# Two hybrid blocks on one core: the first block's attention turns its probabilities two query tiles behind the scores instead of one

## The chip, the cores and the metric

The kernel runs on one core of one Trainium2 chip. The metric is the device time of one execution in microseconds (us). Each time quoted as a median comes from several executions; the profile comes from one further execution, and has its own time. The engines of a core are called PE (TensorE, with PEld for its weight loads), DVE (VectorE), ACT (ScalarE), POOL (GpSimd) and SP (SyncE, which issues the DMAs). Each engine works through its own queue in order, and waits at the head of it for what the instruction needs.

## The reference, cut to what matters

The program is a block of two layers (`first_block`) followed by a second block with a recurrent part, two attentions and 32 experts. The change lies in the attention of the first block, which each of its two layers runs once, on 528 positions, 4 heads, without a mask:

```python
def mla_mix(c_q, c_kv, k_r, q_norm_w, w_uq, kv_norm_w, w_ukv, cos, sin):
    ...
    def attend(qb):
        s = jnp.einsum('bqhd,bkhd->bhqk', qb, k).astype(jnp.float32) * scale
        p = jax.nn.softmax(s, axis=-1).astype(v.dtype)
        return jnp.einsum('bhqk,bkhd->bqhd', p, v)
...
mix = jnp.concatenate([y_f * silu(f_gate), y_p * silu(p_gate), y_a * silu(a_gate)], axis=-1)
h = h + mix @ w_out[l]
```

A query and a key have 192 numbers for each head (128 of its own and 64 turned by position), a value has 128. Everything is float32.

## The kernel before

**Precision.** A product in float32 is made of three matmuls (`mm3`, L183 to L185): each operand is split into a high and a low part (`split`: ACT copies to the high part at L196, DVE subtracts at L197), and the products high x high, high x low and low x high are added up in PSUM. So each split tile is ready twice: the high part when ACT is done, the low part one DVE instruction later.

**One layer** (`layer`, L323) makes the input projections, then the attention, then the output projection. The attention loops over 4 heads `h` and, for each, over query tiles `i` of 128 positions: five tiles in layer 0 (528 positions, the last tile has 16) and four in layer 1 (512 positions).

- `scores` (L489) writes one tile's scores with ten matmuls (L183 to L185, and L498, L499 for the turned half) into a `pp` tile in PSUM; there are two `pp` buffers. DVE takes the maximum (L501, L502), ACT the exponential (L504), DVE the reciprocal and the product (L506, L507), which gives the probabilities `e` in a slab of SBUF. The `pp` buffer is free again when ACT has read it.
- `transpose_p` (L512) turns `e` with five transposes on PE (L523) into the PSUM tile `pt`, of which there is **one** buffer, and splits it into `pth` and `ptl` (a `big` tile; L196, L197). The next tile can be turned when DVE has read `pt`.
- `outputs` (L529) multiplies the turned probabilities of two or three query tiles with the values, 15 matmuls into a `p1` tile, and gates the result into `ys` (L536). It runs after query tile 1 (part 0) and after the last one (part 1).
- `finish` (L611) is `transpose_p` and, where due, `outputs`, and at a head's end the split of `ys` into `mix[4 + h]`.

**What fills the gaps.** A list of generators, `fillers`, holds independent work of the layer: the query and key projections of the next heads (`qk`), and the gates and the Fourier and pooling mixes (`a_gate`, `fp_gate`). `fill(n)` draws n steps from it; how many after each score tile is a table (`STEPS_1`, L63). After the last head `fill(100)` draws the rest. Then the output projection starts: for each of its 8 column tiles it takes `mix` in the order 2, 0, 4, 5, 6, 1, 3, 7, so that `mix[7]`, the last head's, comes last.

**What sets the order.** The program order is that of the Python code, but the framework's scheduler sorts the instructions of each engine once, at build time, by their place in the code and by its own guess of when they are ready. On the chip each queue then runs strictly in that order.

Of the kernel before, what the change touches and what calls it, by code (L numbers as in the profile page):

```python
# [127 lines left out]
def body(ctx, tc, a, out, stop=None, dbg=None):  # L128
# [61 lines left out]
    def slab(dt=F32, n=L):  # L190
        return sl.tile([128, L + 16], dt, name="slab")[:, :n]
# [23 lines left out]
    with ExitStack() as c1:  # L215
# [7 lines left out]
        def ppt():  # L223
            return pp.tile([128, 2, 512], F32, name="pp")

        def ptt():
            return pt_.tile([128, 1024], F32, name="pt")

        def p1t():
            return p1_.tile([128, 512], F32, name="p1")  # L230
# [92 lines left out]
        def layer(l, w0, X, acc, after):  # L323
# [111 lines left out]
            def a_gate(h):  # L435
                t = slab(n=LQ)
                sa[h] = t
                yield from gate_g(1728 + 128 * h, t)
                a_done[h] = True
# [35 lines left out]
            def qk(h):  # L475
                hp, r, r2 = h // 2, slice(64 * (h % 2), 64 * (h % 2) + 64), slice(64 - 64 * (h % 2), 128 - 64 * (h % 2))
                wq = weights(3, [(0, uq[:, 192 * h:192 * h + 128])])
                wk = weights(2, [(0, ukv[:, 256 * h:256 * h + 128])])
                qh, ql = slab(F32R, LQ), slab(F32R, LQ)
                yield from proj_g(wq, Q, lambda p, f: split(p, f(qh), f(ql)))  # L480
                kf = slab()
                yield from proj_g(wk, KV, lambda p, f: V.tensor_tensor(f(kf), p, f(Rkv), op=OP.mult))
                kh, kl = split(kf)
                qs = slab(F32R, LQ)
                ACT(qs[r], qr[hp][r], AF.Copy)
                V.tensor_tensor(qs[r2], qr[hp][r], qs[r].bitcast(F32), op=OP.subtract)
                heads[h] = (qs, qh, ql, kh, kl)
# [24 lines left out]
            def transpose_p(h, i, e):  # L512
                t0, n = TQ[i]
                part = int(t0 >= 256)
                nq = LQ - 256 if part else 256
                if (h, part) not in pts:
                    pts[h, part] = big.tile([128, 2720], F32R, name="big")
                pt = pts[h, part]
                pth = pt[:, :5 * nq].rearrange("p (j q) -> p j q", j=5)
                ptl = pt[:, 1360:1360 + 5 * nq].rearrange("p (j q) -> p j q", j=5)  # L520
                t = ptt()
                for j, (k0, _) in enumerate(TK):
                    nc.tensor.transpose(t[:106, j * 128:j * 128 + n], e[:n, k0:k0 + 106], ident[:n, :n])  # L523
                tv = t[:106, :640].rearrange("p (j q) -> p j q", j=5)[:, :, :n]
                qo = slice(t0 - 256 * part, t0 - 256 * part + n)
                split(tv, pth[:106, :, qo], ptl[:106, :, qo])
                return pth, ptl
# [10 lines left out]
            def fp_gate(m):  # L538
                yield from (fourier, fourier, pool, pool)[m](m % 2)
                t = slab(n=LQ)  # L540
                yield from gate_g(256 + 128 * m if m < 2 else 768 + 128 * (m - 2), t)
                V.scalar_tensor_tensor(t, yf[m][:, q0:], 0.5, t, op0=OP.mult, op1=OP.mult)
                mix[m] = split(t, n=LQ)
# [7 lines left out]
            for m in range(2):  # L551
                p = ptt()
# [9 lines left out]
            for m in range(2):  # L562
# [7 lines left out]
                p = ppt()  # L570
# [18 lines left out]
            for j, (t0, n) in enumerate(TK):  # L589
                p = p1t()  # L590
# [7 lines left out]
            for pr in range(2):  # L598
                for i, nm in enumerate(("c64", "s64")):
# [5 lines left out]

            fillers.extend([qk(1), fp_gate(0), qk(2)] + [a_gate(2), fp_gate(2)][::2 * l - 1]
                           + [qk(3), a_gate(3), fp_gate(1), fp_gate(3)])
            prev = None
            ys = {}

            def finish(h, i, e):  # L611
                pth, ptl = transpose_p(h, i, e)
                if i in (1, NT - 1):
                    fill()
                    if h not in ys:
                        while not a_done[h]:
                            fill()
                        ys[h] = slab(n=LQ)
                    outputs(h, int(i > 1), pth, ptl, ys[h])
                    if i == NT - 1:  # L620
                        mix[4 + h] = split(ys[h], n=LQ)

            for h in range(4):
                for i in range(NT):
                    while h not in heads:
                        fill()
                    e = scores((h, i, heads[h]))
                    fill(int(STEPS_1[l][h][i]))
                    if prev is not None:
                        finish(*prev)  # L630
                    prev = (h, i, e)
            fill(100)
            wo = w_rows(l, 0)
            finish(*prev)

            order = (2, 0, 4, 5, 6, 1, 3, 7)
            for m in range(8):
# [55 lines left out]
    with ExitStack() as c2:  # L693
# [359 lines left out]
        prev = None  # L1053
        for h in range(8):
# [4 lines left out]
            for i in range(4):  # L1059
                e = scores(h, i)  # L1060
# [5 lines left out]
                prev = (h, i, e)  # L1066
# [86 lines left out]
        prev = None  # L1153
        for h in range(4):
            if h < 3:
                fillers.append(q_head(h + 1))
            for i in range(4):
                e = xscores(h, i)
# [5 lines left out]
                prev = (h, i, e)  # L1164
# [33 lines left out]
        for t in range(len(ring) - 4, len(ring)):  # L1198
            q, e, hf = ring[t][0]
# [494 lines left out]
    with tc.manual_schedule(engines={mybir.EngineType.PE}):  # L1694
# [6 lines left out]
        h = combine(0, up_products(0, "u"), s_)  # L1701
        hT_ = None
        for pr in range(1, NP):
# [38 lines left out]
            h = combine(pr, up_products(pr, "u"), s_)  # L1742
            if pr == NP - 2:

                fnw = wk_.tile([128, 4 * GE * CAP], F32, name="sel")[:, :D]
                for c in range(2):
                    p = ptt()
# [135 lines left out]
```

## Time and profile before

| | us |
|---|---|
| median of 3 executions (1424.39 to 1425.71) | 1425.4 |
| the profiled execution, its own time | 1425.72 |
| its span, first to last instruction | 1423.9 |
| PE busy in the span | 1353.4 (95%) |
| DVE, ACT, POOL busy | 683.4, 555.1, 440.1 |
| attention of layer 0 in the trace | from about 117 to 232 |
| attention of layer 1 in the trace | from about 376 to 481 |

A matmul's bar in the trace is longer than its share of PE, since matmuls overlap: bars of about 0.28 us start about 0.12 us apart. Where the trace prints a wait in brackets, it counts from the modelled end of the matmul before, so the start is later than it would have been by about 0.15 us more than the figure in brackets.

### The profile page before, as it was taken

The page shows a single profiled execution, that of the slowest core. Times are in us where ns is not written, and L with a number is a line of the kernel's source. Part 1 is how long each engine was busy: PE and PEld are TensorE (multiplying, and loading weights), DVE is VectorE, ACT ScalarE, POOL GpSimd, SP SyncE. Part 2 cuts the span into 40 slices and gives each one's busy share as a digit, 9 for nine tenths or more (in the row PEclk, how much of TensorE's full clock was granted, in tenths as well). Part 3 has the DMA queues.
Part 4 walks back from the last instruction along what each step waited for, and adds up shares of the span by engine and source line. Part 5 has one row for each costly group of instructions (what it writes and reads, how often), then busy time and mean ns, then how long its engine had stood idle before and what let it go on. Part 6 is the DMA issues. An engine that isn't in the chain of part 4 may idle for free.

```text
span 1423.9 us, 21255 instructions
## 1 busy us (share of the span) xinstructions
PE 1353.4 (95%) x8236; PEld 1018.1 (71%) x8236; DVE 683.4 (48%) x1305; ACT 555.1 (39%) x1048; POOL 440.1 (31%) x363
## 2 busy tenths in 40 slices
PE   6999999999999999989999999979999999999996
PEld 5998999999899997767876788863454354354343
DVE  5656775455677636777766244252213123132224
ACT  5355554334555562667755344421111110111113
POOL 3432223743222488464477432512000000000002
PEclk9999999999999999999999999989999999999998
DMA  6321112332211242313345122959999999999994
GB/s 202 96 75 40 49 52 84 97 97 66 56 42 58 69 125 81 90 52 120 103 127 175 38 63 91 347 200 382 423 403 423 422 422 423 422 420 422 422 418 154
DMA packets 159288, 279.32 MB, mean 196 GB/s; under 512 B 15568, under 2 KB 127440, under 8 KB 135120
## 3 DMA queue, kind: packets, MB, share of 16 engines
q1 hardware_dynamic: 159184, 277.92, 53.0%
q8 instruction: 66, 1.08, 0.3%
q14 instruction: 38, 0.31, 0.1%
HBM read 275.79 MB, written 2.10 MB: 195 GB/s over the span
## 4 chain that ended last, share of the span: by engine, by line
PE 59%; DVE 7%; DMA 3%; ACT 2%; issue 1%; POOL 1%; DVEq 0%; SPq 0%; POOLq 0%; ACTq 0%
PE pga L1530 7%; PE pgb L1530 7%; PE pm L184 5%; PE pm L185 5%; PE pm L183 5%; PE pgs L1621 4%; PE pgz L1580 3%; PE pgy L1580 3%; PE pgs L1352 3%; PE p L183 2%; PE p L184 2%; PE p L185 2%; DMA ring<-in_expert_gate_w_dram 1%; DMA ring<-in_expert_up_w_dram 1%; DVE slab L197 1%
## 5 line engine op out<-in xcount | busy, mean ns | idle before, releaser
L177 POOL TENSOR_TENSOR wl<-wraw,wh 128x512 fp32r<-128x512 f32 (+1 forms) x248 | 328.1, 1332 | 457.1 <-ACT wh L176 425.2
L176 ACT ACTIVATE wh<-wraw 128x512 fp32r<-128x512 f32 (+1 forms) x248 | 150.6, 616 | 212.6 <-PE pm L184 49.8
L183 PE MATMUL pp<-slab,wh 128*128 128x264 f32 (+1 forms) x536 | 154.8, 290 | 7.6 <-ACT wh L176 6.8
L184 PE MATMUL pp<-slab,wh 128*128 128x264 f32 (+1 forms) x536 | 155.7, 291 | 2.9 <-DVE slab L204 2.7
L185 PE MATMUL pp<-slab,wl 128*128 128x264 f32 (+1 forms) x536 | 154.8, 289 | 1.0 <-POOL wl L177 1.0
L1788 POOL TENSOR_TENSOR ring<-xtok,sel 128x512 f32<-128x512 f32 x4 | 5.0, 1282 | 406.2 <-DVE xtok L1623 406.2
L185 PE MATMUL pm<-slab,wl 128*128 128x512 f32 (+1 forms) x320 | 121.5, 381 | 5.6 <-POOL wl L177 5.5
L184 PE MATMUL pm<-slab,wh 128*128 128x512 f32 (+1 forms) x320 | 120.9, 378 | 2.2 <-DVE slab L197 2.2
L183 PE MATMUL pm<-slab,wh 128*128 128x512 f32 (+1 forms) x320 | 121.1, 380 | 0.0
L183 PE MATMUL p<-slab,wh 128*128 128x264 f32 (+1 forms) x400 | 115.7, 289 | 3.3 <-DVE rs L247 1.6
L1530 PE MATMUL pga<-ring,xT 128*64 128x512 f32 x504 | 116.1, 596 | 0.0
L1530 PE MATMUL pgb<-ring,xT 128*64 128x512 f32 x512 | 113.7, 592 | 0.3 <-DMA ring<-in_expert_up_w_dram 0.3
L185 PE MATMUL p<-slab,wl 128*128 128x264 f32 (+1 forms) x400 | 113.1, 283 | 0.0
L184 PE MATMUL p<-slab,wh 128*128 128x264 f32 (+1 forms) x400 | 112.8, 282 | 0.0
L183 PEld LDWEIGHTS pp<-slab,wh 128*128 128x128 f32 x536 | 103.6, 194 | 8.0 <-ACT wh L176 6.8
L184 PEld LDWEIGHTS pp<-slab,wh 128*128 128x128 f32 x536 | 103.4, 193 | 4.7 <-DVE slab L204 4.2
L185 PEld LDWEIGHTS pp<-slab,wl 128*128 128x128 f32 x536 | 103.8, 194 | 1.5 <-POOL wl L177 1.5
L1530 PEld LDWEIGHTS pgb<-ring,xT 128*64 128x64 f32 x512 | 37.0, 137 | 73.6 <-issue 71.4
L1590 DVE SCALAR_TENSOR_TENSOR yl<-pgy,wcol,yh 128x512 fp32r<-128x512 f32 x16 | 12.0, 751 | 158.2 <-ACT yh L1589 158.2
L1530 PEld LDWEIGHTS pga<-ring,xT 128*64 128x64 f32 x504 | 35.4, 137 | 66.1 <-issue 65.6
L183 PEld LDWEIGHTS p<-slab,wh 128*128 128x128 f32 x400 | 75.5, 189 | 5.1 <-issue 1.7
L184 PEld LDWEIGHTS p<-slab,wh 128*128 128x128 f32 x400 | 75.4, 189 | 0.0
(412 smaller groups left out, 3007.6 us busy)
## 6 DMA issues: line engine op xcount, KB each, us to landing
ring<-in_expert_gate_w_dram SPq DMA_DIRECT2D x63, 1024.0 KB, 17.7
ring<-in_expert_up_w_dram SPq DMA_DIRECT2D x62, 1024.0 KB, 16.2
ring<-in_expert_down_w_dram SPq DMA_DIRECT2D x56, 1024.0 KB, 17.0
wraw<-in_w_in_dram SPq DMA_DIRECT2D x108, 256.0 KB, 2.9
wraw<-in_w_out_dram SPq DMA_DIRECT2D x48, 256.0 KB, 2.9
wraw<-in_xk_w_dram SPq DMA_DIRECT2D x16, 256.0 KB, 2.9
wraw<-in_xv_w_dram SPq DMA_DIRECT2D x16, 256.0 KB, 2.6
wraw<-in_xq_w_dram SPq DMA_DIRECT2D x16, 256.0 KB, 2.9
```

The lines of the kernel that those rows point to most:

```text
L176: ACT(h, raw, AF.Copy)
L177: G.tensor_tensor(lo, raw, h.bitcast(F32), op=OP.subtract)
L183: mm(ps, lh, rh, start=first, stop=False)
L184: mm(ps, lh, rl, start=False, stop=False)
L185: mm(ps, ll, rh, start=False, stop=last)
L197: V.tensor_tensor(lo, x, h.bitcast(F32), op=OP.subtract)
L1352: mm(p, h3[:, i, 128 * k:128 * k + 128], sl_[i], start=i == 0 and z == 0, stop=i == 3 and z == 1)
L1530: mm(p[64 * z:64 * z + 64], xt[:, k, CAP * (q + z):CAP * (q + z) + 64], W(src, 2 * pr + z, k), start=k == 0, stop=k == KT - 1)
L1580: mm(ps[c // 512][64 * z:64 * z + 64, c % 512:c % 512 + n], hT_[:, k, 64 * z:64 * z + 64], W("d", 2 * pr + z, k, c, n), start=k == 0, stop ...
L1590: V.scalar_tensor_tensor(yl, p, w[:rows, 0:1], yh.bitcast(F32), op0=OP.mult, op1=OP.subtract)
L1621: mm(p, t[:, 128 * i:128 * i + 128], y, start=q == 0, stop=q == len(ys) - 1)
L1788: G.tensor_tensor(y[i][:, :512], xtok[:, i, :512], fnw[:, :512], op=OP.mult)
```

## The change

The loop over query tiles kept one finished score tile back (`prev`) and called `finish` on it after the next tile's scores. Now `prev` is a list that keeps two tiles back: `finish` is called on tile n after the scores of tile n + 2, over the heads' borders too. After the last head's scores and `fill(100)` two tiles are left to finish instead of one. Nothing is computed otherwise, and no buffer is added.

```diff
-            prev = None
+            prev = []
...
                     e = scores((h, i, heads[h]))
                     fill(int(STEPS_1[l][h][i]))
-                    if prev is not None:
-                        finish(*prev)
-                    prev = (h, i, e)
+                    prev.append((h, i, e))
+                    if len(prev) > 2:
+                        finish(*prev.pop(0))
             fill(100)
             wo = w_rows(l, 0)
-            finish(*prev)
+            for p in prev:
+                finish(*p)
```

The built order of POOL and of SP is the same before and after. On PE, DVE and ACT it differs only inside the two attentions; from the output projections on, and in the whole second block, it is the same. Three places follow, each with PE's order before and after. Numbers behind a tile's name count the tiles of a program, so they differ between the two; what counts is which instruction stands behind which.

**Layer 0, from head 0 to head 1.** Before, PE's queue after the scores of head 1's second query tile (`pp_1787`): five transposes of head 0's last tile (16 positions), twelve matmuls of a key projection (`p1_1731`, `p1_1739`), then the scores of the third tile (`pp_1825`).

```order
L499 MATMUL pp_1787<-slab_777,slab_1499 128x264
L523 MATMUL pt_1747<-tab_63,slab_1657 106x16 x5
L183 MATMUL p1_1731<-slab_467,wh_1674 128x264
...
L185 MATMUL p1_1739<-slab_538,wl_1675 128x264
L183 MATMUL pp_1825<-slab_1495,slab_1407 128x264
```

After, the same score tiles are `pp_1747` (second), `pp_1816` (third) and `pp_1910` (fourth):

```order
L523 MATMUL pt_1739<-tab_63,slab_1561 106x128 x5
L185 MATMUL pp_1747<-slab_1486,slab_1408 128x264
...
L499 MATMUL pp_1747<-slab_777,slab_1490 128x264
L183 MATMUL pp_1816<-slab_1486,slab_1407 128x264
...
L499 MATMUL pp_1816<-slab_777,slab_1490 128x264
L523 MATMUL pt_1782<-tab_63,slab_1648 106x16 x5
L183 MATMUL pp_1910<-slab_1486,slab_1407 128x264
```

Three score tiles now follow each other, with ten transposes and no key projection between them; the key projection stands ahead of them.

**Layer 1, head 1.** Before, PE's queue around the turning of head 1's third tile (`pt_5109`): 15 matmuls of head 1's first output part (`p1_5026`) and the pooling mix (`p1_5061`) stand ahead of it, and a gate projection (`p1_5080`) behind.

```order
L184 MATMUL p1_5026<-big_4965,big_4453 128x256
L185 MATMUL p1_5026<-big_4965,big_4454 128x256
L183 MATMUL p1_5061<-slab_5007,slab_4509 128x256
L184 MATMUL p1_5061<-slab_5008,slab_4509 128x256
L185 MATMUL p1_5061<-slab_5007,slab_4509 128x256
L523 MATMUL pt_5109<-tab_63,slab_4988 106x128 x2
L183 MATMUL p1_5080<-slab_2815,wh_4914 128x256
```

After, the second tile is turned into `pt_5067` and the third into `pt_5155`; `pp_5108` and `pp_5163` are the scores of head 2's first and second tile:

```order
L498 MATMUL pp_5108<-slab_3914,slab_4878 128x264
L499 MATMUL pp_5108<-slab_3915,slab_4878 128x264
L523 MATMUL pt_5067<-tab_63,slab_4862 106x128 x5
L183 MATMUL pp_5163<-slab_4874,slab_4768 128x264
L523 MATMUL pt_5155<-tab_63,slab_4979 106x128 x2
L183 MATMUL p1_5054<-slab_2815,wh_4885 128x256
```

Two turnings now stand with a single matmul between them, and the first output part comes behind both.

**Layer 0, the end of the attention.** Before, PE's queue behind the last output part of the last head (`p1_2732`): matmuls of the output projection (`pp_2765`, `pp_2833`) with parts of `mix` that are ready, until `slab_2749`, the high part of `mix[7]`, is read.

```order
L185 MATMUL p1_2732<-big_2657,big_1319 128x272
L183 MATMUL pp_2765<-slab_2700,wh_2714 128x264
...
L184 MATMUL pp_2833<-slab_2486,wh_2755 128x264
L183 MATMUL pp_2765<-slab_2749,wh_2720 128x264
L185 MATMUL pp_2833<-slab_2485,wl_2756 128x264
```

After:

```order
L185 MATMUL p1_2732<-big_2695,big_1319 128x272
L185 MATMUL pp_2833<-slab_2691,wl_2756 128x264
L183 MATMUL pp_2765<-slab_2749,wh_2712 128x264
L183 MATMUL pp_2833<-slab_2749,wh_2761 128x264
L184 MATMUL pp_2765<-slab_2750,wh_2712 128x264
```

Eleven matmuls stood between the last output matmul and the first that reads `mix[7]`, and 18 ahead of the first that reads its low part (`slab_2750` after); now it is one, and three.

## Rows read from the trace of the kernel before

**Rows 1.** The page: the span, and busy time, share and instructions of PE.

```profile
span 1423.9 us, 21255 instructions
PE 1353.4 (95%) x8236; PEld 1018.1 (71%) x8236; DVE 683.4 (48%) x1305; ACT 555.1 (39%) x1048; POOL 440.1 (31%) x363
```

**Rows 2.** Busy time by stretch (length, then us busy, instructions), clock, DMA share, GB/s.

```profile
117.00:160.00 43.00, 40.93 (x312) 38.08 (x311) 31.72 (x72) 25.06 (x53) 8.94 (x8) 1.00 0.18 46
160.00:210.00 50.00, 50.00 (x415) 48.85 (x414) 34.84 (x76) 24.61 (x52) 12.20 (x10) 1.00 0.19 53
450.00:482.00 32.00, 29.39 (x235) 28.03 (x234) 22.08 (x52) 13.86 (x28) 5.16 (x4) 1.00 0.17 50
```

**Rows 3.** PE's waits in layer 0's attention: us in total, times, longest.

```profile
PE pp L183 <- ACT slab L504: 1.1, 3, 0.4
PE pt L523 <- DVE big L197: 0.7, 1, 0.7
PE p L184 <- DVE slab L197: 0.6, 1, 0.6
```

**Rows 4.** PE in order of time, head 0 to 1: start, us, tile [idle before].

```profile
145.23 0.71 PE L523 MATMUL pt<-tab,slab 128*106 128x128 f32 x5
...
149.04 0.43 PE L523 MATMUL pt<-tab,slab 16*106 16x16 f32 x5 [0.69 <-DVE big L197]
...
151.52 0.39 PE L183 MATMUL pp<-slab 128*128 128x264 f32 x1 [0.39 <-ACT slab L504]
...
155.65 0.39 PE L184 MATMUL p<-slab 128*128 128x264 f32 x1 [0.56 <-DVE slab L197]
...
157.45 0.39 PE L183 MATMUL pp<-slab 128*128 128x264 f32 x1 [0.43 <-ACT slab L504]
```

**Rows 5.** The same view, layer 1's last two heads.

```profile
456.73 0.76 PE L523 MATMUL pt<-tab,slab 128*106 128x128 f32 x5 [0.94 <-DVE big L197]
...
469.97 0.39 PE L184 MATMUL p<-big 106*128 106x256 f32 x1 [0.62 <-DVE big L197]
...
479.80 0.50 PE L183 MATMUL pp<-slab,wh 128*128 128x256 f32 x2 [0.82 <-ACT slab L196]
480.53 0.39 PE L184 MATMUL pp<-slab,wh 128*128 128x256 f32 x1 [0.23 <-DVE slab L197]
```

**Rows 6.** One turning with ACT and DVE free: PE, ACT, DVE in order of time.

```profile
474.17 0.75 PE L523 MATMUL pt<-tab,slab 128*106 128x128 f32 x5
...
474.96 0.71 ACT L196 ACTIVATE big<-pt 106x640 fp32r<-106x640 f32 x1 [1.71 <-PE pt L523]
...
475.70 0.82 DVE L197 TENSOR_TENSOR big<-pt,big 106x640 fp32r<-106x640 f32 x1 [1.59 <-ACT big L196]
```

**Rows 7.** One score tile with DVE and ACT free: last matmul, maximum, exponential.

```profile
219.11 0.29 PE L499 MATMUL pp<-slab 128*128 128x264 f32 x1
...
219.44 0.71 DVE L501 TENSOR_REDUCE st<-pp 128x1 f32<-128x528 f32 x1 [0.19 <-PE pp L499]
...
220.49 0.79 ACT L504 ACTIVATE slab<-pp,st,rqs 128x528 f32<-128x528 f32 x1 [2.90 <-DVE st L502]
```

**Rows 8.** End of layer 0: last output matmul, gating, split, first reads of it.

```profile
230.34 0.29 PE L185 MATMUL p<-big 106*128 106x272 f32 x1
...
230.66 0.44 DVE L536 SCALAR_TENSOR_TENSOR slab<-p,slab 128x272 f32<-128x272 f32 x1 [1.23 <-PE p L185]
...
231.14 0.65 ACT L196 ACTIVATE slab<-slab 128x528 fp32r<-128x528 f32 x1 [2.44 <-DVE slab L536]
...
231.82 0.71 DVE L197 TENSOR_TENSOR slab<-slab 128x528 fp32r<-128x528 f32 x1 [0.71 <-ACT slab L196]
...
232.58 0.39 PE L184 MATMUL pp<-slab,wh 128*128 128x264 f32 x1
```

**Rows 9.** Busy time by stretch, as Rows 2, between the blocks' last attention and the experts.

```profile
930.00:940.00 10.00, 6.06 (x41) 5.28 (x40) 4.86 (x16) 3.04 (x5) 3.84 (x9) 0.79 0.62 230
940.00:950.00 10.00, 6.51 (x34) 6.40 (x34) 8.44 (x30) 2.93 (x8) 0.00 (x0) 0.52 0.70 295
```

## The prediction

> **What bounds the kernel now.** I read the page first: PE is busy for 1353.4 of 1423.9 us [rows 1], so time is lost where PE waits, and won only where such a wait goes. Then the busy time by stretch: from 160 to 210 us, the middle of layer 0's attention, PE starts 415 instructions in 50 us without a gap, 0.12 us each [rows 2]. This is the price of one matmul in all that follows, and nothing in the change alters the number of matmuls. In both attentions DVE and ACT are busy for 43% to 75% of the time and POOL and the DMA for far less [rows 2], so POOL's and SP's queues, which keep their order, wait for nothing new.
>
> Then I read PE's waits in the attentions, for what there is to win. In layer 0 they are 1.1 + 0.7 + 0.6 = 2.4 us, five waits [rows 3]; four of the five come in 9 us, where head 0 passes into head 1 [rows 4]. In layer 1 the large ones come in the last two heads: 0.94, 0.62, 0.82 and 0.23 us [rows 5]. Each start is later by 0.15 us than the bracket says, as told with the table; I count starts, so 0.69 is 0.84.
>
> What to see is who ends these waits. The transposes (L523) wait for DVE at L197, that is for the one `pt` buffer: the tile turned before must be split first [rows 3 to 5]. The scores wait for ACT at L504: with two `pp` buffers, the tile two back must have its exponential. Two waits are for splits of the pooling mix or of `mix[7]`. No transpose waits for its own probabilities (that would be DVE at L507). So the wait that turning two tiles back relieves, for a softmax that is not finished, is not among them; the two it meets are of buffers, and these keep their number.
>
> **The change, part by part.** Three prices come first. A turning with free engines: transposes at 474.17, ACT's part done at 475.67, DVE's at 476.52: 2.35 us until the next tile can be turned, 1.5 us until the high part can be used [rows 6]. In a crowd, with other work ahead on ACT and DVE: 145.23 to 149.04, 3.8 us [rows 4]. A score tile with free engines: last matmul at 219.11, exponential done at 221.28, 2.2 us until its `pp` buffer is free [rows 7]. Five transposes hold PE for about 0.5 us, 0.4 with 16 positions.
>
> *The ends*, for which the order is plainest. After the last scores two tiles must be finished, with the same store of matmuls to cover them: 42 of the output projection read no `mix[7]` and fit into the two `pp` buffers. In layer 0 the chain behind the last output matmul is 230.34 to 232.58, 2.24 us: gating, ACT's split, DVE's split [rows 8]. Now 18 matmuls (2.16 us) lie in it, so it costs nothing. In the new order three are left there (0.36 us), since the others went ahead to cover the extra turning: 15 x 0.12 = **1.8 us** more. The last small turning stands 14 matmuls behind the one ahead: 0.5 + 14 x 0.12 = 2.2 against 2.35, another 0.1. Sum +1.9, between 1.4 and 2.4, as the rest of DVE's queue falls. In layer 1 the waits of the end are now 0.62 + 0.82 + 0.23, with 3 x 0.15 2.1 us [rows 5]. In the new order three tiles instead of two are turned behind the last scores. By cover: the first output part gets 4 matmuls between high and low part, the second 2, so each waits some 0.7 us; the end keeps one matmul instead of three, 0.24 more on 1.45. That is 3.1 instead of 2.1: **+1.0**, between 0.3 and 2.3 (a whole turning).
>
> *Layer 0, head 0 to 1.* Four starts are late now in this passage, 2.07 + 4 x 0.15 = 2.7 us [rows 4]. In the new order the last tile of head 0 is turned 18 matmuls behind the one before: 0.5 + 2.2 = 2.7 us against 2.35 to 3.8. DVE has the maximum of `pp_1747` (0.7) ahead of the split, so I take 0.6 late. The fourth score tile needs the exponential of the second; between are ten matmuls, the small turning and that 0.6, 2.2 us in all, against 2.2 free and 3.7 with the split of a turned tile ahead of it on both engines (0.71 + 0.82): 0.5 late. Behind it, the next turning and the pooling mix wait for DVE as one of them does now: 1.0. Sum 2.1: **-0.6**, between -2.2 and +1.2.
>
> *Layer 0, head 2 to 3.* One wait of 0.28 + 0.15 now (1.1 less the two of rows 4 [rows 3, 4]). In the new order head 2's last two tiles and head 3's first are turned with 14 and 6 matmuls between; on DVE the maximum, a gate's product and its high-and-low work, about 0.7 each by [rows 7, 8], stand ahead of the small split. PE reaches the third turning 3.5 us behind the first, DVE frees it after some 4.4: 0.9, and 0.6 more for the score tile and the pooling split behind: **+1.1**, between 0 and 2.
>
> *Layer 1, head 1.* Second and third tile are turned with one matmul between. With one `pt` buffer the third waits 2.35 - 0.5 - 0.12 = 1.7 us, or to 3.2 in a crowd; the score matmul between waits for an exponential as long. Now the trace prints no wait in this place. Some of it the pooling mix would have cost anyway: **+1.4**, between 0.8 and 2.5.
>
> *Layer 1, head 2 to 3.* Now 0.94 + 0.15 = 1.1 [rows 5], in an order of turning, 19 matmuls, turning that stays. I let it be 0.5 to 1.1. New behind it: only 7 matmuls stand to the next turning, since the 15 of the output part, ten of which cover it now, come later: 2.35 - 0.5 - 0.84 = 1.0, and 0.4 for the pooling split. 2.0 against 1.1: **+0.9**, between 0 and 2.
>
> *At nothing.* The extra `e` slab held for one tile longer shows as no new wait in front of a score tile; the transposes of the first heads keep 12 or more matmuls of cover. If that cover is too thin, 0.1 to 0.3 us come up in several places, which the upper ends hold.
>
> Sum: 1.9 + 1.0 - 0.6 + 1.1 + 1.4 + 0.9 = **+5.7 us**, on the profiled execution's 1425.72. That lies 0.3 over the median, so 1425.4 + 5.7 = **1431.1**. PE is full behind both attentions and the later order is the same, so I let the delay reach the end whole.
>
> **The rivals.**
>
> *The waits go.* If the buffers' waits are at bottom late softmaxes that crowd DVE, the added distance relieves them all: layer 0's 2.4 + 5 x 0.15 = 3.15 and head 2 to 3 in layer 1, 1.1 [rows 3, 5]. The ends stay, +2.9: -1.35, **1424.1**, not slower. It decides if turned tiles are split in 2.35 us everywhere. Against it: no L507 among the releasers. Even this case is less than 0.2% faster, since the ends give most of it back. 8%.
>
> *The new order evens out.* The passage in layer 0 gains its 2.2, head 2 to 3 costs nothing in either layer, head 1 0.8: 2.9 + 0.8 - 2.2 = +1.5, **1426.9**. For it: the scheduler put the cover where its own guess saw gaps. 18%.
>
> *DVE crowds.* If the turnings that now stand close (five beyond the ends) take 3.8 us and not 2.35, the upper ends hold in half the places: about +9, **1434.5**. For it: four waits in 9 us in the one place that looks like this now [rows 4]. 10%.
>
> *The clock falls.* In all attention stretches the granted clock is 1.00, the 2.4 GHz level, with waits up to 0.94 [rows 2, 5]; between 930 and 950, where PE is busy for 12.6 of 20 us, its mean is 0.79 and 0.52, the 1.2 GHz level for much of it [rows 9]. A new wait of 1.7 us is between the two. Ten us at half the speed cost 5 us: **1436**. 3%. The Trainium skill (TensorE: Matmul & The Clock Gate, "Why this matters for your kernels") asks for no idle gaps between bursts of matmuls because the engine falls back to the half rate behind them; rows 9 agree, and by that rule this case would be the likely one only if waits join up.
>
> *It does nothing.* The built orders differ in both attentions, so only if the queues' slack took it all: 1425.4, 1%.
>
> **How the numbers follow.** The forecast has 60%. A measurement of this kernel can tell about 0.2%, 2.85 us, from no change, so slower begins at 1428.3: the forecast, the crowd and the clock, 73%. Within 0.2% lie the evening out, most of the first rival and the last, 24%. Faster by more would need the ends to cost nothing as well, 3%. The lower end of the range takes half of the evening out, 1426.3; the upper leaves out the clock and half of the crowd, 1434.3.
>
> **What would show it.** In the changed kernel's trace, at layer 0's end some 1.3 us of PE idle ahead of the first matmul that reads `mix[7]`, released by ACT at L196, and 0.4 more released by DVE at L197. In layer 1's head 1, around 420 us, a transpose that waits over 1 us for DVE at L197, or the score matmul ahead of it for ACT at L504. Three close score tiles in layer 0 near 150 us with a wait for L504 ahead of the third. PE's printed waits, now 2.4 us in layer 0 and 2.6 us in layer 1's last two heads [rows 3, 5], should grow to some 10 us in both attentions together. It is wrong if layer 0's end shows no idle, if the waits for L523 shrink, or if the second block's length changes by as much as the attentions'.

## The result and the profile after

The changed kernel takes 1439.17 us in the median of four executions (1437.12 to 1443.14), the kernel before beside it 1424.89 (1423.63 to 1425.71): 1.0102 times, 95% interval 1.0080 to 1.0123. Five more executions, taken later beside the experiments, gave 1437.71 in the median and 1.0075 (1.0062 to 1.0089). The profiled execution took 1440.22 us.

The page of after answers [rows 1]: the same 8236 matmuls, a span longer by 14.5 us, and PE busy 5.7 us longer. PE's busy time grows without more work where the granted clock is lower; rows for this follow with the delays.

```profile
span 1438.4 us, 21257 instructions
PE 1359.1 (94%) x8236; PEld 1021.2 (71%) x8236; DVE 685.1 (48%) x1305; ACT 554.1 (39%) x1048; POOL 440.4 (31%) x363
```

PE's waits in layer 0's attention, 117 to 232 us, the view of [rows 3] (released by, us in total, times, longest). 2.4 us have become 5.4, and the 1.3 us at 237 us shown below come on top, since this attention now ends later. A wait is put down to the instruction that ended last: behind L502 and L467 stands the split of a turned tile (L197), which ended 0.1 us before PE went on.

```profile
PE p L183 <- ACT big L196: 1.1, 2, 0.9
PE pp L183 <- ACT slab L196: 1.0, 1, 1.0
PE pt L523 <- DVE st L502: 0.8, 1, 0.8
PE pp L183 <- ACT slab L504: 0.6, 1, 0.6
PE pt L523 <- DVE big L197: 0.5, 1, 0.5
PE p L184 <- DVE slab L197: 0.5, 1, 0.5
PE p L184 <- DVE slab L467: 0.4, 1, 0.4
...
```

The same view of layer 1's attention, 376 to 496 us, 6.9 us in all (before has 3.1):

```profile
PE pt L523 <- DVE big L197: 1.7, 2, 1.0
PE pp L183 <- ACT slab L504: 1.6, 1, 1.6
PE pp L183 <- ACT slab L196: 1.2, 1, 1.2
PE p L184 <- DVE slab L197: 0.8, 1, 0.8
PE pp L183 <- DVE slab L470: 0.6, 1, 0.6
PE p L184 <- DVE big L197: 0.5, 2, 0.3
...
```

Three places in PE's order of time, as [rows 4, 5]: layer 1's head 1; layer 0's end, with a wait for the split of `mix[3]` at 230 us and two for that of `mix[7]` at 237; and a place in layer 0's head 1 that the prediction has at nothing:

```profile
425.45 0.73 PE L523 MATMUL pt<-tab,slab 128*106 128x128 f32 x5
427.75 0.39 PE L183 MATMUL pp<-slab 128*128 128x264 f32 x1 [1.57 <-ACT slab L504]
427.98 0.38 PE L523 MATMUL pt<-tab,slab 128*106 128x128 f32 x2
```
```profile
230.17 0.39 PE L183 MATMUL pp<-slab,wh 128*128 128x264 f32 x1 [1.01 <-ACT slab L196]
...
235.62 0.29 PE L185 MATMUL p<-big 106*128 106x272 f32 x1
...
237.11 0.51 PE L183 MATMUL pp<-slab,wh 128*128 128x264 f32 x2 [1.08 <-ACT slab L196]
237.85 0.39 PE L184 MATMUL pp<-slab,wh 128*128 128x264 f32 x1 [0.23 <-DVE slab L197]
```
```profile
165.80 0.71 PE L523 MATMUL pt<-tab,slab 128*106 128x128 f32 x5
...
167.70 0.28 PE L185 MATMUL p<-slab,wl 128*128 128x264 f32 x1
168.85 0.38 PE L183 MATMUL p<-big 106*128 106x256 f32 x1 [0.87 <-ACT big L196]
```

**How the loss was placed.** Both kernels start the same number of matmuls, so the start of the n-th in one trace less the start of the n-th in the other is the delay up to there. Its growth over a stretch is what the stretch lost. Worked out from the starts of every trace (stretches by the times of before, us lost against before):

| stretch | after | second trace of after | predicted term |
|---|---|---|---|
| layer 0, head 0 to 1 (131 to 163) | 0.63 | 1.02 | -0.6 |
| layer 0, in heads 1 and 2 (163 to 207) | 2.15 | 2.13 | at nothing |
| layer 0, head 2 to 3 (207 to 225) | 0.63 | 0.62 | +1.1 |
| layer 0, the end (225 to 250) | 2.62 | 2.62 | +1.9 |
| between the layers (250 to 388) | 2.74 | 0.03 | nothing |
| layer 1, head 0 and into 1 (388 to 408) | 0.58 | 0.54 | at nothing |
| layer 1, head 1 (408 to 431) | 1.52 | 1.59 | +1.4 |
| layer 1, in head 2 (431 to 452) | 0.89 | 0.86 | at nothing |
| layer 1, head 2 to 3 (452 to 474) | 1.90 | 0.79 | +0.9 |
| layer 1, the end (474 to 504) | 0.49 | 1.99 | +1.0 |

The two traces agree within 0.1 us wherever PE only waits. They differ in four rows, and there the granted clock differs: it falls to 0.50, the 1.2 GHz level, at 288, 370 and 469 us in the one, and at 155 and 493 us in the other. Taking each row from the trace whose clock stays up, waits cost 6.0 us in layer 0 and 4.3 in layer 1, 10.3 together. What else these rows lost, 3.8 us in the one trace and 1.9 in the other, goes with the falls.

### The profile page after: what moved, and what is told of

The parts are those of the page before. It is cut to its first block, busy times and chain, and to the rows that moved or that the text cites. A ratio compares the mean times of both kernels' runs of the same rounds, so it can differ in the third digit from the quotient of the medians.

```text
span 1438.4 us, 21257 instructions
## 1 busy us (share of the span) xinstructions
PE 1359.1 (94%) x8236; PEld 1021.2 (71%) x8236; DVE 685.1 (48%) x1305; ACT 554.1 (39%) x1048; POOL 440.4 (31%) x363
## 3 DMA queue, kind: packets, MB, share of 16 engines
q8 instruction: 66, 1.08, 0.3%
## 4 chain that ended last, share of the span: by engine, by line
PE 51%; DVE 7%; DMA 6%; ACT 2%; issue 1%; POOL 1%; DVEq 0%; SPq 0%; POOLq 0%; ACTq 0%
PE pgb L1531 6%; PE pga L1531 6%; PE pm L184 5%; PE pm L185 5%; PE pm L183 5%; PE pgs L1622 4%; PE pgz L1581 3%; PE pgy L1581 3%; DMA ring<-in_expert_up_w_dram 3%; PE pgs L1353 3%; DMA ring<-in_expert_gate_w_dram 1%; DMA ring<-in_expert_down_w_dram 1%; DVE slab L197 1%; PE pp L184 1%; PE pp L185 1%
```

## Experiments: where the waits are

Theory A: the loss is waits, it sits in both attentions, and adds up. Rivals: it is the clock, or a part is caught up later.

**Two behind in one layer only**, layer 0 (`l0_only`) or layer 1 (`l1_only`):

```diff
-                    if len(prev) > 2:
+                    if len(prev) > (2 if l == 0 else 1):
```

> Two tiles behind in layer 0 only; layer 1 as before. Theory A (the loss is waits for buffers and for splits in the two attentions, and adds up by layer): the trace of after shows layer 0 longer by 6.0 us (3.4 in the attention, 2.6 at its end), so 1424.9 + 6.0 = 1430.9, between 1429 and 1434 with one or two more falls of the clock of 3.4 us (1.7 each). Rival B (the layers' waits are small and most of the 14.3 is the clock, set off by the new order): clearly off that, either under 1427.5 or over 1435, and no layer's part stands alone. Rival C (a delay in layer 0 is caught up later): under 1428.

> Two tiles behind in layer 1 only; layer 0 as before. Theory A: layer 1's attention is longer by 5.7 us in the trace of after, of which about 1.5 is a fall of the clock at 469 us; so +4.2, 1429.1, between 1427.5 and 1432.5. By A the two excesses, this one and layer 0 only, add up to some 10, and what is missing to 14.3 is the clock. Rival B (most of it is the clock): under 1427.5 where the clock does not fall, and the waits at the score tile of head 1 (1.57 us in after) and at the transposes of heads 2 and 3 (0.69 and 1.01) gone or small.

Measured: 1432.86 us, 1.0044 (1.0027 to 1.0060), and 1433.57 us, 1.0055 (1.0043 to 1.0068), beside 1425.84. The excesses, 7.0 and 7.7, add up to 14.7; after had 14.3 and 12 in its two sets. Stretch by stretch, `l0_only` loses 1.04, 2.13, 0.61 and 2.64 in layer 0 and nothing from there to 504 us; `l1_only` loses nothing in layer 0 and 5.7 in layer 1, where its clock falls once, as in after. Where the clock stays up, the stretches repeat after's to 0.1 us, but for layer 1's end in `l1_only` (0.83 against 0.49). So the loss adds up by layer, and nothing is caught up. In time, `l1_only` lies above A's range of 1427.5 to 1432.5, and the sum is 14.7 where A had some 10 and the clock for the rest: each run has falls of the clock of its own.

**The end as before** (`end_back`): the last head's first tile is finished ahead of the last scores, so one tile is left behind `fill(100)`.

```diff
+                    last = (h, i) == (3, NT - 1)
+                    if last:
+                        finish(*prev.pop(0))
                     e = scores((h, i, heads[h]))
...
-                    if len(prev) > 2:
+                    if len(prev) > (1 if last else 2):
```

> Two tiles behind in both layers, but the first tile of the last head is finished ahead of the last scores, and the second right behind them, so that one tile alone is left behind the last matmuls of the store, as before the change. Theory A: layer 0's end gives back its 2.6 us and layer 1's its 0.2, less about 0.5 in each for two turnings that now stand closer; 1439.2 - 1.8 = 1437.4 by the medians, and the idle of about 1 us that ACT at L196 and DVE at L197 end in layer 0's output projection goes to nothing. Rival D (the end's price is only moved to the last head, where PE waits for the same splits): 1439, with new waits of 1 to 2 us at the last head's transposes.

Measured: 1436.21 us, 1.0077 (1.0064 to 1.0090). Layer 0's end loses 0.02 us instead of 2.62, and neither the row of 230 us above nor those of 237 have a counterpart: PE is busy for 9.88 of the 10 us from 224 to 234. So the 2.6 are the price of finishing two tiles on a store that covers one. Layer 1's end isn't cured: it loses 2.4, with a fall of the clock in it, and the waits for the split of `mix[7]` stay at 1.18 and 0.22. Theory A held, and the price did not move into the stretch ahead of it (0.57 from 207 to 225 us, 0.63 in after).

**What the transposes wait for** (`half_two`, and `half_one` in the kernel before): `pt` in two halves of one PSUM bank each, split one after the other, so that the next turning can start behind the first.

```diff
-            return pt_.tile([128, 1024], F32, name="pt")
+            return pt_.tile([128, 512], F32, name="pta"), pt_.tile([128, 512], F32, name="ptb")
...
-                split(tv, pth[:106, :, qo], ptl[:106, :, qo])
+                for z, js in enumerate((slice(0, 3), slice(3, 5))):
+                    tv = t[z][:106, :(js.stop - js.start) * 128].rearrange("p (j q) -> p j q", q=128)[:, :, :n]
+                    split(tv, pth[:106, js, qo], ptl[:106, js, qo])
```

> Two tiles behind, and the one buffer of the turned tile made of two halves (three key tiles and two), each split by itself, so that the next turning may begin when the first three are split. Theory E (the transposes' waits are for the one buffer): the waits that DVE at L197 ends ahead of transposes, 0.49 and 0.31 us in layer 0 and 0.69 + 1.01 in layer 1, go or fall under 0.2, and the output parts' high halves come 0.3 earlier: some 2.5 us less than after, 1436.5. Rival F (the splits themselves come late, because ACT and DVE do other things first): the waits stay, and the two more instructions for each turned tile make them longer: 1439 to 1441.

> The same halves in the kernel before, one tile behind. Theory E: the transposes' waits of before, 0.69 + 0.56 us in layer 0 and 0.94 in layer 1, go: 1425.3 - 2 = 1423.3. Rival F: they stay, and two more instructions for each turned tile on ACT and on DVE (about 0.2 us each of their fixed part) come ahead of what PE waits for: 1425 to 1428.

Measured: 1434.17 us, 1.0057 (1.0043 to 1.0071), and 1426.86 us, 1.0009 (1.0000 to 1.0018). With two behind, heads 1 and 2 of layer 1 (408 to 452) lose 1.3 us instead of 2.4, layer 0's end 1.4 instead of 2.6, and layer 1's end gains 1.1 where it lost 0.5. But in layer 0's head 0 to 1 it loses 2.16 against 0.63, with a fall of the clock at 158. The waits for DVE at L197 don't all go; some get shorter, others are new (PE's waits from 100 to 260 us):

```profile
PE pta L523 <- DVE big L197: 1.1, 2, 0.8
PE p L184 <- DVE slab L197: 1.0, 1, 1.0
PE p L184 <- DVE big L197: 0.6, 1, 0.6
...
PE ptb L523 <- DVE big L197: 0.4, 1, 0.4
```

So the one buffer is a part of the loss in the changed kernel, as E says. How large a part stays open: the edit also splits the mixes' turned tiles in two and moves the built order. At 168 us, where a mix's split stood ahead of the turned tile's on ACT (next experiment), it now stands behind the first half's, and 166 to 171 us loses 0.4 instead of 1.2. In the kernel before, where turnings mostly stand 20 and more matmuls apart, the same halves win nothing, as F says.

**Queue order on ACT.** At 168 us in after, the first output part waits for the turned tile's high part. ACT in order of time:

```profile
164.99 0.42 ACT L365 ACTIVATE slab<-slab 128x264 f32<-128x264 f32 x1
167.56 0.64 ACT L196 ACTIVATE slab<-slab 128x528 fp32r<-128x528 f32 x1 [2.15 <-DVE slab L542]
168.11 0.69 ACT L196 ACTIVATE big<-pt 106x640 fp32r<-106x640 f32 x1
```

The tile was turned by about 166.3, and ACT had nothing to do. But the split of a mix, which waits 2.15 us for DVE's product, stands ahead of it in the queue. Two ways of writing the mixes' splits later: behind the next turned tile's split (`pt_first_two`, and `pt_first_one` in the kernel before), or behind the next output part (`mix_late`):

```diff
-                mix[m] = split(t, n=LQ)
+                late.append((m, t))
+            def flush():
+                while late:
+                    m, t = late.pop(0)
+                    mix[m] = split(t, n=LQ)
...
                     outputs(h, int(i > 1), pth, ptl, ys[h])
+                    flush()
```

> Two tiles behind, and the high-and-low split of a pooling or Fourier mix is written down behind the next turned tile's split instead of ahead of it; nothing else. In the trace of after the first output part of layer 0's head 1 waits 0.87 us for the turned tile's high part: the split of a mix stands ahead of it on ACT and waits 2.15 us for DVE's product at L542. Theory G (queue order: what waits for DVE on ACT holds up the turned tile behind it): that wait goes, and the one of 0.24 a head later; 0.9 to 1.5 us less than after, 1437.9. Rival H (DVE is the one that is late; with the mix behind, its split waits as long, or the output projection waits for it): no gain, 1439 or more, the wait goes to another line.

> The same writing order in the kernel before, one tile behind. In its trace no output part waits for a turned tile's high part that stands behind a mix. By G little is to win: 1425.3 within 0.7. By H it costs, since the mixes' splits come later and the out-projection reads them: 1426.5 to 1428.

Measured: 1432.47 us (1429.50 to 1442.02), 1.0068 (1.0045 to 1.0091), and 1425.55, 1.0003 (0.9994 to 1.0012). As a test of the place at 168 us the first says nothing, since the scheduler kept the mix ahead there and the trace still has the 0.9. From 368 to 504 us it lost 2.3 us, where after lost 5.4 with a fall of the clock in it; that stretch was not aimed at.

> Two tiles behind, and the high-and-low splits of the Fourier and pooling mixes are written down behind the next output part instead of where the mix is finished, so that in layer 0's head 1 the turned tile's split now stands ahead of the mix's on ACT (in the run before, with the splits behind the turned tile's, the built order had not moved there, and the 0.87 us were still in the trace). Theory G (queue order): the 0.87 us go, and so do other waits of output parts and score tiles for ACT at L196 within the heads; 1 to 2.7 us less than after's 1437.0 at a mean clock of 0.985, so 1434.3 to 1436. Rival H (three turnings of layer 0 then stand 15 and 5 matmuls apart, where they had 18 and 10, and wait for DVE instead): no gain.

Measured: 1437.43 us, 1.0079 (1.0066 to 1.0093). Here the built order did move. ACT around the same turning:

```profile
164.22 0.70 ACT L196 ACTIVATE big<-pt 106x640 fp32r<-106x640 f32 x1 [1.13 <-PE pt L523]
166.33 0.42 ACT L365 ACTIVATE slab<-slab 128x264 f32<-128x264 f32 x1 [1.41 <-DVE slab L364]
166.66 0.63 ACT L196 ACTIVATE slab<-slab 128x528 fp32r<-128x528 f32 x1
```

The turned tile's split comes first, waits only for PE, and the stretch from 166 to 171 us loses 0.3 instead of 1.2, with the same twelve matmuls between the turning and the output part. So G is right for this place. In layer 1, from 388 to 474 us, the loss is 1.4 instead of 3.8 (second trace of after), but there PE's order moved as well: behind the turning at 439 us of after the next one stands 20 matmuls away and waits 0.69 for DVE at L197; in `mix_late` it stands 79 away and doesn't wait. So that gain is not shown to be ACT's order. The median shows little of either, since this kernel's executions had the lowest mean clock of all, 0.9817.

The loss from 193 to 200 us in after, 1.2 us, is of the same kind by its rows:

```profile
193.54 0.71 PE L523 MATMUL pt<-tab,slab 128*106 128x128 f32 x5
193.59 0.79 ACT L504 ACTIVATE slab<-pp,st,rqs 128x528 f32<-128x528 f32 x1 [0.80 <-DVE st L502]
...
195.21 0.69 ACT L196 ACTIVATE big<-pt 106x640 fp32r<-106x640 f32 x1
...
195.34 1.29 DVE L366 SCALAR_TENSOR_TENSOR slab<-slab 128x264 f32<-128x264 f32 x1
...
195.95 0.38 PE L183 MATMUL p<-big 106*128 106x256 f32 x1 [0.24 <-ACT big L196]
...
196.62 0.81 DVE L197 TENSOR_TENSOR big<-pt,big 106x640 fp32r<-106x640 f32 x1
...
197.49 0.38 PE L184 MATMUL p<-big 106*128 106x256 f32 x1 [0.43 <-DVE slab L467]
```

The tile is turned by about 194.0. On ACT an exponential, a weight's copy and a gate's work stand ahead of its split, on DVE the gate's product of 1.29 us, and the output part comes 13 matmuls behind the turning. Its two late starts, 0.24 and 0.43 with 2 x 0.15, are 1.0 of the 1.2. In before the same gate's work stands ahead of this split, but the output part comes behind the next turning, and nobody waits. No run took this place apart.

**The table of cover steps** (`steps_late`), moved by one tile:

```diff
-STEPS_1 = (("22222", "22322", "21222", "21212"), ("2322", "2323", "2333", "3323"))
+STEPS_1 = (("22222", "22232", "22122", "22121"), ("2232", "2232", "3233", "3332"))
```

> Two tiles behind, with the table of cover steps (STEPS_1) moved by one tile, so that the steps ahead of a turning are again those that were ahead of it before the change. Theory I (the loss is a table that was made for one tile behind): 3 us or more less than after, under 1434 at a mean clock of 0.985. Rival E (the turnings crowd on one buffer whatever the table: in the built order two pairs still stand 14 and 6 matmuls apart, one pair of layer 1 has 9 instead of one, another 3): 1436 to 1438.

Measured: 1439.75 us, 1.0100 (1.0085 to 1.0114). Layer 0's end costs 0.75 instead of 2.62, but from 463 to 504 us layer 1 loses 1.3 instead of 0.2, and the median wins nothing. Theory I falls for this one shift of the table; a table made anew was not tried.

**Three cures together** (`two_cured`): halves, `end_back` and `mix_late`.

> Two tiles behind with three cures together: the turned tile's buffer in two halves, the first tile of the last head finished ahead of the last scores, and the mixes' splits behind the output parts. If the loss is made of these three things and they add up: at a mean clock of 0.985 after's 1437.0 less 4.2 (halves), 2.2 (end) and 1 to 2.7 (splits), 1428 to 1429.6. Rival (they are the same waits, cured twice): 1432 or more. Theory of a hidden gain (with the buffers out of the way the distance pays): under 1425.5.

Measured: 1433.36 us (1428.46 to 1433.83), 1.0051 (1.0038 to 1.0064). Its trace, of the fastest execution, loses 2.9 us in layer 0, 0.9 from 368 to 391 us, and gains 1.2 from there to 504, 2.6 in all, of the 10.3 of after. By the median less is gone: at a mean clock of 0.985 the line below makes it 1431.3, between the forecast of three cures that add up (1428 to 1429.6) and the rival's 1432. So a good part of the loss can be taken away, how much is open. What is left is still slower than before, so no run shows a gain from the distance itself; [rows 3 to 5] had no transpose that waited for its own softmax.

## Experiments: the clock

**A pure delay** (`delay`): 42 matmuls in the output projection of layer 0 of the kernel before, whose result nobody reads.

```diff
+                if m == 3 and l == 0:
+                    pd = p1t()[:, :264]
+                    for z in range(42):
+                        mm(pd, w_lag[z % 8][0], mix[2][0][:, :264], start=z == 0, stop=z == 41)
```

> The kernel before with 42 matmuls more in layer 0's output projection, whose result nobody reads: a pure delay of 42 x 0.11 to 0.12 = 4.6 to 5.0 us in a place where PE does not wait. It tells what a shift alone does to all that stands behind. Theory A (the later stages keep their length): 1424.9 + 4.8 = 1429.7, between 1428 and 1431.5. Rival B (a shift alone brings the clock to fall at idle places where it does not fall before, such as those of 0.94 and 1.57 us that POOL and DVE end near 282 and 364 us): over 1431.5, with more falls in the trace than before's. Rival C (the delay is caught up at a transfer or a later wait): under 1428.

Measured: 1432.69 us, 1.0044 (1.0029 to 1.0058): 6.9 more, for a delay that is 5.04 in the trace. The shift stays at 5.04 until 369 us, and is 6.50 behind it. Busy time by stretch (length, us busy and instructions, PEclk, DMA share, GB/s), first before, then delay, each pair from the same work on: PE waits 1.57 us for DVE at L247, and then the clock stays in the one and falls in the other.

```profile
360.00:363.90 3.90, 2.36 (x21) 2.16 (x20) 3.21 (x8) 1.98 (x5) 0.77 (x2) 1.00 0.16 45
364.10:367.40 3.30, 3.05 (x24) 2.76 (x23) 1.15 (x5) 1.71 (x4) 1.22 (x2) 1.00 0.14 40
```
```profile
365.00:368.90 3.90, 2.37 (x21) 2.17 (x19) 3.20 (x8) 1.99 (x5) 0.76 (x2) 1.00 0.20 48
369.10:372.40 3.30, 3.30 (x16) 3.30 (x17) 0.95 (x4) 0.80 (x2) 0.79 (x1) 0.50 0.16 45
```

So Rival B holds for this run. One such fall costs 6.50 - 5.04 = 1.46 us. Another 0.9 comes in the second block, at 752 us by the time of before, and is no clock: PE waits 0.85 us for ACT at L196, where before doesn't wait.

**Other delays, and both kernels again:**

> The kernel before with 42 matmuls more in the output projection of each layer, so 84 in all, whose results nobody reads: 10.1 us by the 5.04 that 42 took in the run with one delay, about what after loses in PE's waits, but without a wait. Theory B2 (part of what the change costs is the clock, which falls at idle places common to both kernels when the work behind a delay comes later): 1425.4 + 10.1 + 1.4 to 3.4 = 1437.5, at a mean granted clock of 0.982 to 0.984, with falls near 370 and 750 us that before does not show. Rival (a delay without waits leaves the clock alone): 1435.5 at 0.986.

> The kernel before with 21 matmuls more in layer 0's output projection: 2.5 us by the 0.12 of one. If any shift costs clock: 1428 + 1.5 = 1429.5 at 0.984. If only waits do: 1428 at 0.986.

> The same with 63 matmuls: 7.6 us. If any shift costs clock: 1433 + 1.5 to 3 = 1435 at 0.983. If only waits do: 1433 at 0.986. If it is the amount of the shift that decides, between these, and with falls at other idle places than after a shift of 5 us.

> The changed kernel, unchanged, for more executions and a second trace. If the clock's part is its own: again 1439 at a mean granted clock of 0.982, with falls near 288, 370 and in layer 1's attention. If it was the luck of four executions: 1436.9 at 0.985. The waits are those of the first trace to 0.1 us in both cases.

> The kernel before, unchanged, for a second trace: 1425.5. If the places of the clock's falls belong to the order of the work, they are at 28, 564, 629, 639 and 936 us again; if they belong to the execution, some move.

| kernel | delay in the trace | median us | over before | mean granted clock |
|---|---|---|---|---|
| before (75 executions, before_again's too) | - | 1425.7 | - | 0.9858 |
| before_again | - | 1425.67 | -0.1 | 0.9864 |
| delay_21 | 2.5 | 1428.53 | 2.7 | 0.9852 |
| delay | 5.0 | 1432.69 | 6.9 | 0.9842 |
| delay_63 | 7.6 | 1436.03 | 10.2 | 0.9832 |
| delay_both | 5.0 + 5.0 | 1436.42 | 10.7 | 0.9857 |
| after, nine executions | (waits) | 1437.9 | 12.2 | 0.9827 |

The rival of `delay_both` held: 10 us in two parts cost no clock. `delay_21` lies between its two forecasts; its trace has one fall, at 366 us, which costs 1.1. But 7.6 us in one part cost 2.6 on top, 0.8 of it the wait at 752 us, and its trace has falls at 289 and 371 us, as the first trace of after has at 288 and 370. Such a place, a PE that waits 0.94 us for POOL ahead of five transposes, is in both kernels alike. In delay_63 and in before, in PE's order of time:

```profile
288.38 0.67 PE L256 MATMUL pt<-tab,rstd 106*128 106x106 f32 x5 [0.94 <-POOL rstd L249]
```
```profile
282.36 0.67 PE L256 MATMUL pt<-tab,rstd 106*128 106x106 f32 x5 [0.93 <-POOL rstd L249]
```

Behind it PEclk is 0.51 in delay_63 and 0.50 in after, against 1.00 in before:

```profile
289.30:292.70 3.40, 3.40 (x18) 3.40 (x18) 2.10 (x4) 1.24 (x2) 0.28 (x1) 0.51 0.49 154
```
```profile
288.30:291.70 3.40, 3.40 (x18) 3.40 (x18) 2.31 (x4) 1.24 (x2) 0.49 (x1) 0.50 0.48 148
```
```profile
282.00:286.00 4.00, 3.64 (x32) 3.64 (x33) 2.07 (x4) 1.25 (x2) 1.55 (x2) 1.00 0.50 143
```

The falls move from execution to execution as well: `before_again` has none near 639, and one at 575 instead of 564.

Inside the attentions the falls go with the new order. All four traces with layer 1's order of the changed kernel (after, after_again, l1_only, end_back) have a fall there, at 469, 493, 461 and 488 us. The nine traces with layer 1's old order have none between 380 and 500. Of the five with the new order altered one has, `mix_late`; `pt_first_two` and `steps_late` have none, with waits of 1.56 and 1.44 us there, so a long wait alone does not bring a fall. In after, PE is busy for 1.74 us between 465.5 and 468.9, and then the clock falls:

```profile
465.50:468.90 3.40, 1.74 (x14) 1.32 (x12) 3.40 (x6) 1.87 (x3) 0.29 (x1) 1.00 0.50 149
469.30:472.50 3.20, 3.20 (x17) 3.12 (x17) 1.78 (x5) 1.43 (x4) 0.00 (x0) 0.50 0.00 0
```

**Both parts together.** A straight line through all executions of the kernels, with one slope for all and a level for each, gives 0.73 us (error 0.05) for 0.001 of mean granted clock. At equal clock after is 10.5 us (error 0.45) over before; by stretches the waits were 10.3. The clock part of the nine executions is (0.9858 - 0.9827) x 730 = 2.3 us. 10.5 + 2.3 = 12.8, and the means differ by 12.7. The line is no better than about 0.9 us: it gives the delays of 21, 42, 63 and 42 + 42 matmuls 2.4, 5.6, 9.3 and 10.7, where their traces have 2.5, 5.9, 8.4 and 10.1, the wait at 752 us included. By the same line `l0_only` is 5.9 over, `l1_only` 6.2, `half_two` 6.9, `mix_late` 8.1, `end_back` 8.9. For `two_cured` it gives 5.3, twice the 2.6 of its trace; this stays unexplained.

**What stays open.** Why one shift brings falls and another doesn't, and how much of the 2.3 us is due to the new waits and how much to the shift. One fall in layer 1, 1.1 to 1.5 us, goes with the new order, and so does one near 155 us in layer 0 (in two of the four traces with layer 0's new order unaltered, in none of nine with the old), where it costs some 0.4 us. The others lie at places that both kernels have.

## Why the prediction was right in kind and too small

The direction and the reason were right: no wait for a softmax was there to win, and the change pays with buffer waits and a barer end. The time, 1439.17 against 1431.1, lies above the range of 1426.3 to 1434.3. PE's printed waits in both attentions grew from 5.5 us to 13.6, where some 10 were announced.

- **The ends**, +1.9 and +1.0: 2.6 and 0.5, together 3.1 against 2.9. In the first, the announced chain shows 1.08 and 0.23 of printed wait for 1.3 and 0.4, with 2 x 0.15 some 1.6 us. Ahead of the low part of `mix[7]` there stood 16 matmuls, not the 18 that the sum and the text on the change have, so the term was 13 x 0.12 = 1.6: this mechanism was right. The other 1.0 us came at 230 us and was not in the term: PE drew on its store earlier, and the 22nd of its matmuls reads `mix[3]`, whose split on ACT was still waiting for DVE at L542. `end_back` took both away. In the second, the 1.45 in the sum are 0.82 + 0.23 + 2 x 0.15 = 1.35.
- **Layer 1, head 1**, +1.4: 1.5 to 1.6. Of the two signs named, it is the score matmul between the two turnings that waits, 1.57 for ACT at L504.
- **Layer 1, head 2 to 3**, +0.9: 0.8 where the clock stays up, 1.9 where it falls.
- **Layer 0, head 2 to 3**, +1.1: 0.6, within its bounds.
- **Layer 0, head 0 to 1**, -0.6: +0.6. The wait of 0.60 for L504 came ahead of the score tile as announced, but the passage did not get faster. Within its bounds.
- These terms sum to 6.7 against 5.7. **The step that failed is "At nothing".** The stretches outside the named places lost 2.15 in layer 0, 0.6 and 0.9 in layer 1, 3.6 us in all. The step asked how many matmuls of cover stand behind each turning, and found 12 or more. It did not ask what stands ahead of the turned tile's split on ACT and DVE. At 168 us the cover was there, twelve matmuls, and ACT was idle, but a mix that was waiting for DVE held the queue; `mix_late` shows it for that place. At 193 to 200 us the rows read the same way, untested, and the 1.0 us at 230 us are a split that waits on ACT too. For the places in layer 1 the cause stays open in part. The upper ends were meant to hold such places, at 0.1 to 0.3 each; they were 0.6 to 1.2 each.
- **"I let the delay reach the end whole"** failed by 2.3 us (nine executions), 3 to 4 in the first four. The falls come, but the rival at 3% priced the clock as one long stretch at half speed behind a wait of 1.7. What came were short ones, at waits of 0.8 to 1.6 us and at idle places of the old order that were reached at another time. The Trainium skill (TensorE: Matmul & The Clock Gate, "Why this matters for your kernels") asks for no long idle gaps between bursts of matmuls. Here falls came behind short waits, 0.8 to 1.6 us, as well, and the rows at 282 and 288 us show that the same idle is followed by a fall in one execution and not in another.
- **The waits go**, 8%, falls: the printed waits more than doubled. **Evens out**, 18%, falls: the passage lost 0.6 where it should gain 2.2, and head 1 lost 1.5. Of the forecast times the clock's 1436 comes nearest, but its one long stretch did not come. **DVE crowds**, +9, is near the 10.3 us of the waits alone, but not by 3.8-us turnings: the named places beyond the ends came to 3.6, their forecast to 2.8.
- The sign on the second block held: from 504 us to the end the two traces of after differ from before by +1.2 and -0.7 us, and `before_again` by +0.8.

## What to carry to other kernels

When a step of a software pipeline is moved, list for every queue that it uses what now stands ahead of it, and whether that waits for another engine; cover counted on the consumer's engine says nothing on that. If no wait in the trace is for the latency that a deeper pipeline hides, look for what the depth costs: here it cost 10 us of waits, 2.6 of them at one end, where one more step has to be drained on the same store of cover. Compare two kernels by the start of the n-th matmul, and at equal mean clock, before a difference of a few us is put down to the change.

## What was not expected of the hardware

A delay of 5.04 us without any wait cost 6.9 us in the median, and one of 7.6 us cost 10.2, and their traces show the granted clock falling at idle places of 0.94 and 1.57 us where the undelayed kernel's stayed at 1.00, 1.3 to 1.5 us each, and a new wait of 0.8 us in the second block. The mean granted clock of one and the same kernel went from 0.978 (1442.02 us) to 0.990 (1429.50 us) between executions of `pt_first_two`. Printed waits, in contrast, repeat to 0.1 us from trace to trace.
